# First expert's weights and x for h in 512 KB pieces behind weight tiles; last output pass split contiguously; gate products after both affinity transposes

## The chip, the cores and the metric

The kernel runs on one core of a Trainium2 chip. The metric is device microseconds of one execution; three executions of the kernel before took 1984.89 us in the median (1982.02 to 1988.62).

## The reference, cut to what matters

One trunk layer, all in float32: 256 latent and 256 context tokens of width 2048.

```python
mod = silu(c) @ w_mod + b_mod                       # shift, scale, gate for both halves of the layer
u = modulate(rmsnorm(tokens)) @ w_in                # 512 tokens, w_in 2048 x 11328
y = concat(ssd_branch(u[..., :D_SSM_IN]), short_conv_branch(u[..., D_SSM_IN:]))
h = x + g1 * (y @ w_out)[latent tokens]             # w_out 4096 x 2048
f = modulate(rmsnorm(h), sh2, sc2)
aff = softmax(f @ w_router)                         # 256 x 16
gates, idx = top_k(aff.T, 32)                       # each of 16 experts takes 32 tokens
xe = f[idx]
ye = (silu(xe @ w_gate) * (xe @ w_up)) @ w_down * gates   # per expert: 2048x1024, 2048x1024, 1024x2048
out = rmsnorm(h + g2 * scatter_add(ye, idx))
```

The expert weights are 402 MB of the 641 MB that the kernel moves.

## The kernel before, in words

**Dense part.** The products with w_in and w_out take their weights in tiles of 512 KB. `split_tile` (L84 to L113) makes one: it loads the tile into one of three `raw` buffers on SP's queue (L94), ScalarE casts it to a rounded half `whi` (L104), VectorE subtracts that to get `wlo` (L105), and TensorE makes three products of the halves (L339 and L336 for w_in, L826 and L883 for w_out), for a half tile of w_in 24 matmuls of 256 columns. After each tile's subtraction `split_tile` also issues what is due: postponed steps (`at_tick`), and rows of w_mod on the POOL queue at a set pace (`pace_`, 130 rows per 100 tiles, 105 from w_out on), each a 256 KB load `mraw` and one VectorE step (L406).

**Output projection.** The residual h (256 x 2048) starts as x, two loads of 1 MB (L752). Two passes over w_out give the columns 0 to 1024 and 1024 to 1536, with tokens as output rows (L826). The last pass gives columns 1536 to 2048 transposed (L878 to L886): there the weight tile is the operand that TensorE loads (LDWEIGHTS on PEld) and the token data move. Its four groups of 128 columns are every fourth column, so `split_tile` is called with `fours`: ScalarE and VectorE read the tile with a stride of four elements and write the halves grouped, and each matmul loads 128 neighbouring columns. Here too a tile has three products, 24 matmuls of 256 columns, and there are 16 tiles.

**Routing.** Logits `pl` (L891, L894), softmax per half of the tokens (`aff`), two transposes into `pa` (L919), and from it the search for each expert's 32 tokens on VectorE. Beside it TensorE makes `pt`, 16 small products that spread the gate g2 over rows (L923), which ScalarE copies to `g2r` (L925); four matmuls `warm` (L929) read `g2r`; the search's first result `bd` goes to TensorE in `pi` (L952).

**Experts.** 16 experts one after the other; each reads gate and up tiles of 2 MB (L1036, matmuls `gu` L1042) and down tiles (L1067, L1070). A tile's place comes from `wtile` and a list of slots: `ebig`, `abig`, `ebig`, four times `abig`, two `mbig` for the first nine, then a ring of the same. The first expert's tiles have slots that come free during the dense part (a slot `abig` holds halves of an activation until its last matmul), so they can be loaded before the experts begin: gate and up 0 to 3 alternating (below g0, u0, g1, u1, g2, u2, g3, u3), and 1 MB of the down weights (L1067, tile `e`).

**Order.** The engines run in the order that a scheduler writes down for each at build time, by readiness and by priority (`high_priority`); `issue_after` holds an instruction's place until another is placed. SP's queue starts its loads in that order: a load whose buffer isn't free holds all behind it.

Of the kernel before, what the change touches and what calls it, by code (L numbers as in the profile page):

```python
# [14 lines left out]
P = 128  # L15
# [11 lines left out]
RATE, RATE_OUT = 130, 105  # L27


@with_exitstack  # L30
def layer(ctx: ExitStack, tc: tile.TileContext, x, c, cx, c_ctx, w_mod, b_mod, norm_mix_w, w_in,
# [27 lines left out]
    def sbank(name="s"):  # L59
        return bank("s", 4, name)  # L60
# [22 lines left out]
    pace = [None]  # L83
# [4 lines left out]
    def split_tile(src, k0, c0, n, kn, fours=False):  # L88


        with tc.high_priority(offset=ahead[0]):
            w = raw_tile()
            wv = w.rearrange("p a b -> p (a b)")[:, 0:kn * n].rearrange("p (a b) -> p a b", a=kn)
            nc.sync.dma_start(wv, src.rearrange("(k p) c -> p k c", p=P)[:, k0:k0 + kn, c0:c0 + n])  # L94
            hi = wp.tile([P, 1024], F32R, name="whi", tag="whi", bufs=3)
            lo = wp.tile([P, 1024], F32R, name="wlo", tag="wlo", bufs=3)
            hv = hi[:, 0:kn * n].rearrange("p (a b) -> p a b", a=kn)
            lv = lo[:, 0:kn * n].rearrange("p (a b) -> p a b", a=kn)
            if fours:
                wf = wv.rearrange("p a (c i) -> p a i c", i=4)  # L100
                hf, lf = (v.rearrange("p a (i c) -> p a i c", i=4) for v in (hv, lv))
            else:
                wf, hf, lf = wv, hv, lv
            nc.scalar.copy(hf, wf)  # L104
            sub = nc.vector.tensor_tensor(lf, wf, hf.bitcast(F32), op=OP.subtract)  # L105
        tick[0] += 1
        with tc.issue_after(sub.ins):
            for x in sorted(y for y in due if y[0] <= tick[0]):
                due.remove(x)
                x[2]()  # L110
            if pace[0]:
                pace[0]()
        return hv, lv  # L113
# [313 lines left out]
    steps = mod_rows()  # L427
    n_rows, owed = [0], [0]

    def mod_rows_to(n):  # L430
        while n_rows[0] < n and next(steps, 0) is None:
            n_rows[0] += 1

    def pace_(rate, top):
        def fn():
            owed[0] += rate
            mod_rows_to(min(top, n_rows[0] + owed[0] // 100))
            owed[0] %= 100
        return fn
# [294 lines left out]
    yt = ebig().rearrange("p (k l) -> p k l", l=L)  # L734
    for j in range(1, 4):
        sc_block(j, gp, yt[:, 4 * j - 4:4 * j])
        for jj in ((0, 1) if j == 1 else (j,)):
            sq = squares(ysc[jj])
            if jj == 0:
                nc.gpsimd.tensor_copy(sums, sq)  # L740
            else:
                nc.gpsimd.tensor_tensor(sums, sums, sq, op=OP.add)
    mod_rows_to(12 * KT)
    pace[0] = pace_(RATE_OUT, 16 * KT)
    scx.close()
    h = hp_.tile([P, 2, D], F32, name="h")
# [4 lines left out]
    for t in range(2):  # L751
        nc.sync.dma_start(h[:, t], x[P * t:P * t + P, :])  # L752
# [122 lines left out]
    ov = [ob[i // 2][:, L * (i % 2):L * (i % 2) + L] for i in range(4)]  # L875
    for k0 in range(0, 2 * KT, 2):
        hi, lo = split_tile(w_out, k0, C3, 512, 2, True)
        end = k0 == 2 * KT - 2  # L878
        todo = [(i, x) for x in products(k0, 2, hi, lo) for i in range(4)]
        if end:  # L880
            todo.sort(key=lambda x: x[0])
        for i, (j, pi, yy, w) in todo:
            nc.tensor.matmul(ov[i], w[:, j, P * i:P * i + P], yy, start=(k0 + j == 0 and pi == 0 and i % 2 == 0),  # L883
                             stop=(end and j == 1 and pi == 2), skip_group_check=True)
# [28 lines left out]
    for t in range(2):  # L913
# [5 lines left out]
        nc.tensor.transpose(pa[0:NE, P * t:P * t + P], aff[:, t], ident)  # L919
    pt = sbank("pt")  # L920
    for q in range(4):
        for j in range(4):
            nc.tensor.matmul(pt[32 * q:32 * q + 32, P * j:P * j + P], g2c[:, 4 * q + j:4 * q + j + 1].to_broadcast([P, 32]),  # L923
                             ident, start=True, stop=True)
    nc.scalar.copy(g2r, pt)  # L925
# [73 lines left out]
    for e_ in range(NE):  # L999
# [32 lines left out]
        for k0 in range(0, KT, 4):  # L1032
            wt = []
            for w in (w_gate, w_up):
                t = wtile()
                nc.sync.dma_start(t.rearrange("p (a b) -> p a b", a=4),  # L1036
                                  w[e_].rearrange("(b p i) f -> p b i f", p=P, i=4)[:, k0 // 4])
                wt.append(t)
# [126 lines left out]
```

## Time and profile before

| | us |
|---|---|
| median of three executions | 1984.89 |
| the profiled execution | 1986.1 |
| its span | 1984.2 |
| dense part, to the end of the last pass | 0 to 1031 |
| routing, to the first expert's matmuls | 1031 to 1058 |
| experts | 1058 to 1984 |

PE was busy for 83% of the span, DVE for 46%, ACT for 27%, POOL for 9%; the DMA engines moved 641.11 MB, 323 GB/s over the span. The granted TensorE clock was 0.913 of full speed in the mean. The stages in the last three rows are read from the timeline of TensorE: the last matmul of L883, the first of L1042. Windows of the trace are read with four things in mind: how long an engine was busy, how many instructions it ran (so the spacing of like ones), what clock TensorE was granted, and what share of the 16 DMA engines was busy.

### The profile page before, as it was taken

How to read it: one execution, taken by the hardware profiler on the slowest of the kernel's cores; microseconds unless marked ns; L12 is line 12 of the kernel's file. 1: busy time of each engine (PE TensorE's matmuls, PEld its weight loads, DVE VectorE, ACT ScalarE, POOL GpSimd, SP SyncE). 2: the span in 40 equal slices, each digit the busy share in tenths (PEclk: the TensorE clock that was granted, in tenths of full speed). 3: DMA queues.
4: the chain of work that ended last, by engine and by line, in shares of the span. 5: the costliest groups of instructions: out<-in, count | busy, mean ns of one | idle time of the engine just before them, and what ended most of it. 6: DMA issues, size and time to landing. Idle time of an engine off the chain costs nothing.

```text
span 1984.2 us, 25476 instructions
## 1 busy us (share of the span) xinstructions
PE 1650.6 (83%) x10340; PEld 1014.4 (51%) x10340; DVE 914.7 (46%) x1387; ACT 532.2 (27%) x847; POOL 184.7 (9%) x314
## 2 busy tenths in 40 slices
PE   7999999999999799989988767667666767676686
PEld 5677997778699799867872111111111111111122
DVE  2457985778688688878743111111101111101113
ACT  4323554664666343434530000000000000000002
POOL 1000110212022233312100000000000000000000
PEclk9999999999999899999979887887878888988888
DMA  9964783546376989888768999999999999999996
GB/s 356 404 225 138 227 266 108 160 134 192 99 223 213 328 286 320 281 300 305 259 256 339 421 427 428 427 427 428 427 427 427 428 427 427 427 427 427 428 426 249
DMA packets 145813, 641.11 MB, mean 323 GB/s; under 512 B 16265, under 2 KB 34950, under 8 KB 120480
## 3 DMA queue, kind: packets, MB, share of 16 engines
q1 hardware_dynamic: 124528, 570.19, 73.9%
q0 software_dynamic: 20880, 68.25, 10.0%
q8 instruction: 81, 1.33, 0.3%
q10 hardware_dynamic: 288, 1.05, 0.1%
q14 instruction: 36, 0.29, 0.0%
HBM read 637.34 MB, written 2.10 MB: 322 GB/s over the span
## 4 chain that ended last, share of the span: by engine, by line
DMA 43%; PE 41%; issue 7%; DVE 5%; ACT 2%; POOL 1%; SPq 1%; POOLq 0%; ACTq 0%; DVEq 0%
DMA abig<-in_w_up_dram 21%; PE g L339 12%; PE g L336 11%; DMA ebig<-in_w_up_dram 6%; PE gu L1042 5%; DMA ebig<-in_w_down_dram 4%; DMA abig<-in_w_down_dram 3%; DMA mraw<-in_w_mod_dram 3%; DMA raw<-in_w_in_dram 2%; PE g L826 2%; DMA mwt<-in_w_down_dram 2%; PE yd L1075 2%; DMA mwt<-in_w_up_dram 2%; PE pm L248 1%; PE py L679 1%
## 5 line engine op out<-in xcount | busy, mean ns | idle before, releaser
L339 PE MATMUL g<-abig,whi 128*128 128x256 f32 x2048 | 373.2, 286 | 12.8 <-ACT whi L104 10.9
L105 DVE TENSOR_TENSOR wlo<-raw,whi 128x1024 fp32r<-128x1024 f32 x241 | 309.5, 1287 | 139.8 <-ACT whi L104 138.2
L104 ACT CAST whi<-raw 128x1024 fp32r<-128x1024 f32 x241 | 270.4, 1124 | 372.8 <-DMA raw<-in_w_out_dram 84.7
L1042 PE MATMUL gu<-abig,xe 128*32 128x512 f32 x1200 | 246.3, 778 | 117.8 <-DMA abig<-in_w_up_dram 106.1
L339 PEld LDWEIGHTS g<-abig,whi 128*128 128x128 f32 x2048 | 319.3, 193 | 19.0 <-ACT whi L104 11.2
L339 PE MATMUL g<-abig,wlo 128*128 128x256 f32 x1024 | 285.0, 286 | 2.1 <-DVE wlo L105 2.1
L1047 DVE SCALAR_TENSOR_TENSOR hid<-hid,gu 64x512 f32<-64x512 f32 x16 | 10.9, 679 | 482.2 <-ACT hid L1046 482.2
L336 PE MATMUL g<-abig,whi 128*128 128x512 f32 (+1 forms) x672 | 216.2, 400 | 3.7 <-ACT abig L320 2.0
L1046 ACT ACTIVATE hid<-gu 64x512 f32<-64x512 f32 x16 | 9.5, 591 | 722.9 <-PE gu L1042 722.9
L406 DVE SCALAR_TENSOR_TENSOR macc<-mraw,csl,macc 128x512 f32<-128x512 f32 x240 | 185.4, 773 | 28.1 <-DMA mraw<-in_w_mod_dram 26.0
L339 PEld LDWEIGHTS g<-abig,wlo 128*128 128x128 f32 x1024 | 194.5, 193 | 4.2 <-DVE wlo L105 3.2
L1042 PEld LDWEIGHTS gu<-abig,xe 128*32 128x32 f32 x1200 | 53.6, 133 | 277.1 <-DMA abig<-in_w_up_dram 135.7
L401 POOL DMA_DIRECT2D mraw<-in_w_mod_dram x256 | 138.1, 540 | 586.3 <-DVE macc L406 307.4
L1042 PE MATMUL gu<-ebig,xe 128*32 128x512 f32 x432 | 117.2, 801 | 45.5 <-DMA ebig<-in_w_up_dram 44.3
L1042 PE MATMUL gu<-mwt,xe 128*32 128x512 f32 x416 | 121.4, 862 | 33.8 <-DMA mwt<-in_w_up_dram 32.6
L336 PEld LDWEIGHTS g<-abig,whi 128*128 128x128 f32 (+1 forms) x672 | 122.8, 186 | 40.6 <-issue 9.2
L336 PE MATMUL g<-abig,wlo 128*128 128x512 f32 (+1 forms) x336 | 131.2, 394 | 0.0
L826 PE MATMUL g<-whi,abig 128*128 128x512 f32 x384 | 112.8, 397 | 6.1 <-ACT whi L104 5.4
L1089 DVE TENSOR_TENSOR m<-m,g 128x512 f32<-128x512 f32 x112 | 70.2, 683 | 77.5 <-PE g L1085 77.4
L1042 PEld LDWEIGHTS gu<-ebig,xe 128*32 128x32 f32 x432 | 24.5, 138 | 118.8 <-DMA ebig<-in_w_up_dram 58.6
L826 PEld LDWEIGHTS g<-whi,abig 128*128 128x128 f32 x384 | 72.8, 191 | 23.5 <-ACT whi L104 7.3
L1023 POOL DMA_DIRECT2D h<-in_final_norm_w_dram x1 | 0.6, 578 | 848.4 <-PE pt L1005 848.4
(339 smaller groups left out, 1801.5 us busy)
## 6 DMA issues: line engine op xcount, KB each, us to landing
raw<-in_w_in_dram SPq DMA_DIRECT2D x177, 512.0 KB, 4.7
abig<-in_w_up_dram SPq DMA_DIRECT2D x38, 2048.0 KB, 36.1
abig<-in_w_gate_dram SPq DMA_DIRECT2D x37, 2048.0 KB, 38.7
mraw<-in_w_mod_dram POOLq DMA_DIRECT2D x256, 256.0 KB, 4.8
abig<-in_w_down_dram SPq DMA_DIRECT2D x30, 2048.0 KB, 36.3
big<-in_w_mod_dram SPq DMA_DIRECT2D x32, 1024.0 KB, 10.5
raw<-in_w_out_dram SPq DMA_DIRECT2D x64, 512.0 KB, 5.2
mwt<-in_w_down_dram SPq DMA_DIRECT2D x16, 2048.0 KB, 34.7
```

The source lines that it names most:

```text
L104: nc.scalar.copy(hf, wf)
L105: sub = nc.vector.tensor_tensor(lf, wf, hf.bitcast(F32), op=OP.subtract)
L248: nc.tensor.matmul(pm[32 * q:32 * q + 32, o:o + n], cst[:, k], w[:, k - k0], start=(k < 4), stop=(k >= KT - 4), skip_group_check=True)
L336: nc.tensor.matmul(banks[ct][0:ncol], st, a[q][:, kk], start=beg, stop=end)
L339: nc.tensor.matmul(banks[ct // 2][0:ncol, o:o + L], st, a[q][:, kk, L:2 * L], start=beg and ct % 2 == 0, stop=end, skip_group_check=True)
L401: nc.gpsimd.dma_start(w, w_mod[P * k:P * k + P, c0:c0 + 512])
L406: nc.vector.scalar_tensor_tensor(acc, w, cs, acc, op0=OP.mult, op1=OP.add)
L679: nc.tensor.matmul(oo, l, r, start=(i == 0), stop=(i == 3), skip_group_check=True)
L826: nc.tensor.matmul(ob[nn * t + m], yy[:, P * t:P * t + P], w[:, j, 512 * m:512 * m + 512], start=(k0 + j == order[0] and pi == 0), stop=(k ...
L1042: nc.tensor.matmul(gu[32 * q:32 * q + 32], xe[:, k], wt[q // 2][:, 1024 * kk + 512 * (q % 2):1024 * kk + 512 * (q % 2) + 512], start=(k == ...
L1075: nc.tensor.matmul(yd[32 * q:32 * q + 32], hidT[:, j, 32 * (c // 2):32 * (c // 2) + 32], parts[i][:, 512 * q:512 * q + 512], start=(c == 0 ...
L1089: nc.vector.tensor_tensor(av, h[:, t, 512 * q:512 * q + 512] if e_ == 0 else av, pc[q], op=OP.add)
```

## The change

A generator `first_weights` issues the first expert's seven tiles g0, u0, g1, u1, g2, u2, g3 in quarters of 512 KB, after g0 the 1 MB of down weights in two halves and x for h in four pieces of 512 KB: 34 pieces in all. They are issued by `feed`, which `split_tile` calls with `issue_after(load.ins)`, so each stands behind the load of the weight tile before it: from the twelfth tile of the short convolution's last three blocks on, half a piece per tile up to 10, then from the eighth tile of w_out's first pass on up to 18, and from the eighth of the last pass on one piece per tile up to 34; `first_to(34)` issues what is left. The slots are the same, and so are the bytes. `counted` makes the pace of w_mod's rows usable for both.

```diff
...
-    def split_tile(src, k0, c0, n, kn, fours=False):
+    def split_tile(src, k0, c0, n, kn):
...
-            nc.sync.dma_start(wv, src.rearrange("(k p) c -> p k c", p=P)[:, k0:k0 + kn, c0:c0 + n])
+            load = nc.sync.dma_start(wv, src.rearrange("(k p) c -> p k c", p=P)[:, k0:k0 + kn, c0:c0 + n])
...
-            if fours:
-                wf = wv.rearrange("p a (c i) -> p a i c", i=4)
-                hf, lf = (v.rearrange("p a (i c) -> p a i c", i=4) for v in (hv, lv))
-            else:
-                wf, hf, lf = wv, hv, lv
-            nc.scalar.copy(hf, wf)
-            sub = nc.vector.tensor_tensor(lf, wf, hf.bitcast(F32), op=OP.subtract)
+            nc.scalar.copy(hv, wv)
+            sub = nc.vector.tensor_tensor(lv, wv, hv.bitcast(F32), op=OP.subtract)
...
+        with tc.issue_after(load.ins):
+            if feed[0]:
+                feed[0]()
...
+    def first_weights():
+        for n, slot in enumerate([ebig, abig, ebig] + [abig] * 4):
+            first.append(abig(F32) if slot is abig else slot())
+            src = (w_gate, w_up)[n % 2][0].rearrange("(b p i) f -> p b i f", p=P, i=4)[:, n // 2]
+            for i in range(4):
+                nc.sync.dma_start(first[n][:, 1024 * i:1024 * i + 1024], src[:, i])
+                yield
+            if n == 0:
+                first8.append(e8())
+                src = w_down[0, 4 * P:6 * P].rearrange("(p i) n -> p i n", i=2)[:, 0]
+                for i in range(2):
+                    nc.sync.dma_start(first8[0][:, 1024 * i:1024 * i + 1024], src[:, 1024 * i:1024 * i + 1024])
+                    yield
+                for t in range(2):
+                    for c in range(0, D, 1024):
+                        nc.sync.dma_start(h[:, t, c:c + 1024], x[P * t:P * t + P, c:c + 1024])
+                        yield
...
+    at_tick(12, lambda: feed.__setitem__(0, feed_(FEED, 10)))
...
+    at_tick(8, lambda: feed.__setitem__(0, feed_(FEED, 18)))
...
-    for t in range(2):
-        nc.sync.dma_start(h[:, t], x[P * t:P * t + P, :])
+    first_to(10)
...
+    at_tick(8, lambda: feed.__setitem__(0, feed_(FEED_LAST, 34)))
...
-        hi, lo = split_tile(w_out, k0, C3, 512, 2, True)
+        hi, lo = split_tile(w_out, k0, C3, 512, 2)
...
-            nc.tensor.matmul(ov[i], w[:, j, P * i:P * i + P], yy, start=(k0 + j == 0 and pi == 0 and i % 2 == 0),
+            nc.tensor.matmul(ov[i], in_fours(w[:, j])[:, i], yy, start=(k0 + j == 0 and pi == 0 and i % 2 == 0),
...
-        nc.tensor.transpose(pa[0:NE, P * t:P * t + P], aff[:, t], ident)
-    pt = sbank("pt")
...
+        turned = nc.tensor.transpose(pa[0:NE, P * t:P * t + P], aff[:, t], ident)
+    with tc.issue_after(turned.ins):
+        pt = sbank("pt")
...
```

SP's queue in the tail of w_in, before: `raw` are weight tiles of 512 KB, 128x4096 is 2 MB, 128x2048 is 1 MB.

```order
L94 DMA raw<-in_w_in_dram 128x2x512 x101
L752 DMA h<-in_x_dram 128x2048
L94 DMA raw<-in_w_in_dram 128x2x512
L752 DMA h<-in_x_dram 128x2048
L1036 DMA ebig<-in_w_gate_dram 128x4096
L1067 DMA e_10260<-in_w_down_dram 128x2048
L94 DMA raw<-in_w_in_dram 128x2x512 x50
```

The same place after; 128x1024 is 512 KB.

```order
L95 DMA raw<-in_w_in_dram 128x2x512 x101
L744 DMA ebig<-in_w_gate_dram 128x1024
L95 DMA raw<-in_w_in_dram 128x2x512
L744 DMA ebig<-in_w_gate_dram 128x1024 x3
L95 DMA raw<-in_w_in_dram 128x2x512
L750 DMA e_6341<-in_w_down_dram 128x1024 x2
L95 DMA raw<-in_w_in_dram 128x2x512 x2
L754 DMA h<-in_x_dram 128x1024
L95 DMA raw<-in_w_in_dram 128x2x512 x2
```

Of the 5 MB that stood around one weight tile, 1.5 MB of g0 now stand between two tiles, the 1 MB of down weights behind the next, and the four pieces of h (the first is shown) each behind two more.

SP's queue in the second half of the last pass, before: u1, g2, u2 and g3 in 2 MB.

```order
L94 DMA raw<-in_w_out_dram 128x2x512 x25
L1036 DMA abig<-in_w_up_dram 128x4096
L94 DMA raw<-in_w_out_dram 128x2x512 x3
L1036 DMA abig<-in_w_gate_dram 128x4096
L94 DMA raw<-in_w_out_dram 128x2x512 x3
L1036 DMA abig<-in_w_up_dram 128x4096
L94 DMA raw<-in_w_out_dram 128x2x512
L1036 DMA abig<-in_w_gate_dram 128x4096
```

After:

```order
L744 DMA abig<-in_w_up_dram 128x1024
L95 DMA raw<-in_w_out_dram 128x2x512 x2
L744 DMA abig<-in_w_gate_dram 128x1024 x2
L95 DMA raw<-in_w_out_dram 128x2x512
L744 DMA abig<-in_w_gate_dram 128x1024
L95 DMA raw<-in_w_out_dram 128x2x512
L744 DMA abig<-in_w_gate_dram 128x1024
L95 DMA raw<-in_w_out_dram 128x2x512
L744 DMA abig<-in_w_up_dram 128x1024 x4
L744 DMA abig<-in_w_gate_dram 128x1024 x4
```

The last weight tile stood behind u2; now u2 and g3 stand behind it, and pieces of g2 between the last four tiles. (In the first w_out pass, u0 and g1 likewise turn from two loads of 2 MB into pieces: u0's four still in a row, g1's behind the next tiles as 2, 1 and 1.)

TensorE's order in the routing, before:

```order
L919 MATMUL pa<-ident,aff 16x128
L923 MATMUL pt<-ident,mods 32x128 x15
L919 MATMUL pa<-ident,aff 16x128
L923 MATMUL pt<-ident,mods 32x128
L929 MATMUL warm<-g2r,ident 128x512 x4
L952 MATMUL pi__10081<-bd,ones 128x128
```

After:

```order
L950 MATMUL pa<-ident,aff 16x128 x2
L955 MATMUL pt<-ident,mods 32x128 x16
L961 MATMUL warm<-g2r,ident 128x512 x4
L984 MATMUL pi__10113<-bd,ones 128x128
```

All 16 gate products now stand behind the second transpose; `warm` and `pi` stay behind them.

## Rows read from the trace of the kernel before

**Rows 1.** The profile page: the chain that ended last, shares of the span by engine.

```profile
DMA 43%; PE 41%; issue 7%; DVE 5%; ACT 2%; POOL 1%; SPq 1%; POOLq 0%; ACTq 0%; DVEq 0%
```

**Rows 2.** Stretches: PE, PEld, DVE, ACT, POOL busy (instructions); PE clock; DMA share; GB/s.

```profile
1100.00:1950.00 850.00, 592.82 (x3340) 147.34 (x3340) 123.49 (x224) 24.04 (x46) 0.58 (x1) 0.84 1.01 426
1052.00:1062.00 10.00, 8.61 (x58) 2.46 (x54) 2.50 (x8) 0.59 (x1) 0.00 (x0) 0.83 0.12 48
```

**Rows 3.** Waits of SP's queue from 980 to 1064: waited-for, total us, times, longest.

```profile
SPq L1067 <- PE gu L1042: 27.8, 1, 27.8
```

**Rows 4.** Timeline of SP's queue from 632: start, us, line, load.

```profile
635.58 0.42 SPq L1036 DMA_DIRECT2D ebig<-in_w_gate_dram  x1
636.61 0.39 SPq L94 DMA_DIRECT2D raw<-in_w_in_dram  x1
```

**Rows 5.** Timelines of ACT, DVE and PE at 657; in brackets idle time before, releaser.

```profile
657.19 1.04 ACT L104 CAST whi<-raw 128x1024 fp32r<-128x1024 f32 x1 [14.64 <-DMA raw<-in_w_in_dram]
658.26 1.23 DVE L105 TENSOR_TENSOR wlo<-raw,whi 128x1024 fp32r<-128x1024 f32 x1 [11.45 <-ACT whi L104]
658.28 1.22 PE L339 MATMUL g<-abig,whi 128*128 128x256 f32 x4 [10.95 <-ACT whi L104]
```

**Rows 6.** Stretches around the burst at 635, columns as in rows 2.

```profile
648.00:658.00 10.00, 0.00 (x0) 0.00 (x0) 0.00 (x0) 0.81 (x1) 0.00 (x0) 0.59 0.99 385
658.00:663.00 5.00, 4.68 (x20) 4.39 (x21) 4.70 (x6) 2.32 (x3) 1.08 (x2) 0.50 0.52 150
632.00:664.00 32.00, 21.01 (x154) 20.32 (x153) 19.99 (x32) 7.85 (x11) 8.29 (x12) 0.79 0.88 332
664.00:760.00 96.00, 95.12 (x794) 94.92 (x793) 81.79 (x102) 38.31 (x42) 32.57 (x54) 1.00 0.90 303
```

**Rows 7.** Timelines of SP's queue and PE around g1's load at 860.

```profile
859.98 0.33 SPq L1036 DMA_DIRECT2D ebig<-in_w_gate_dram  x1
874.45 1.60 PE L826 MATMUL g<-whi,abig 128*128 128x512 f32 x4 [4.58 <-ACT whi L104]
```

**Rows 8.** Stretches of the last pass, columns as in rows 2.

```profile
967.00:1031.00 64.00, 56.48 (x418) 54.30 (x417) 42.49 (x38) 33.40 (x25) 4.84 (x9) 0.90 0.68 244
1000.00:1008.00 8.00, 6.58 (x31) 6.37 (x32) 7.89 (x6) 4.46 (x4) 0.00 (x0) 0.58 0.88 343
1024.00:1031.00 7.00, 5.15 (x23) 4.94 (x24) 2.86 (x3) 1.10 (x3) 0.00 (x0) 0.59 0.00 0
```

**Rows 9.** Groups of PE, 967 to 1031: busy us, mean ns | idle before, releaser.

```profile
L883 PE MATMUL g<-abig,whi 128*128 128x256 f32 x255 | 42.0, 301 | 4.4 <-ACT whi L104 4.4
L883 PE MATMUL g<-abig,wlo 128*128 128x256 f32 x128 | 24.1, 305 | 2.8 <-DVE wlo L105 2.8
```

**Rows 10.** Timelines of SP's queue, ACT and DVE at the last two tiles.

```profile
1013.23 0.34 SPq L1036 DMA_DIRECT2D abig<-in_w_up_dram  x1
1013.66 0.67 SPq L94 DMA_DIRECT2D raw<-in_w_out_dram  x1
1022.30 1.99 ACT L104 CAST whi<-raw 128x1024 fp32r<-128x1024 f32 x1 [6.97 <-DMA raw<-in_w_out_dram]
1024.32 1.98 DVE L105 TENSOR_TENSOR wlo<-raw,whi 128x1024 fp32r<-128x1024 f32 x1 [6.11 <-ACT whi L104]
```

**Rows 11.** Timeline and groups of weight loads: strided (L861) and contiguous (L883, L626).

```profile
975.51 0.56 PEld L861 LDWEIGHTS pt<-ident,h 128*128 128x128 f32 x4
975.98 0.20 PEld L883 LDWEIGHTS g<-abig,whi 128*128 128x128 f32 x1
...
L883 PEld LDWEIGHTS g<-abig,whi 128*128 128x128 f32 x256 | 37.4, 208 | 5.7 <-ACT whi L104 4.8 <-issue 0.8
L626 PEld LDWEIGHTS pt<-ident,xs 128*128 128x128 f32 x64 | 8.0, 141 | 5.1 <-issue 3.2 <-PE g L336 0.5 <-PE g L339 0.2
```

**Rows 12.** Timeline of PE in the routing.

```profile
1044.15 3.70 PE L929 MATMUL warm<-g2r,ident 128*128 128x512 f32 x8 [0.67 <-ACT g2r L925]
1048.86 0.34 PE L952 MATMUL pi__10081<-bd,ones 16*128 16x128 f32 x1 [1.01 <-DVE bd L949]
```

More of the change, by code (lines that the diff above doesn't have):

```diff
@@ L27 @@
 RATE, RATE_OUT = 130, 105
+FEED, FEED_LAST = 50, 100
 @with_exitstack
@@ L81, in at_tick @@
         due.append((tick[0] + n, seq[0], fn))
-    pace = [None]
+    pace, feed = [None], [None]
     def raw_tile():
         return wp.tile([P, 2, 512], F32, name="raw", tag="raw", bufs=3)
-    def split_tile(src, k0, c0, n, kn, fours=False):
+    def split_tile(src, k0, c0, n, kn):
         with tc.high_priority(offset=ahead[0]):
@@ L425, in mod_rows, with counted, to, pace_ @@
                 yield
[L427 to L439, printed above, removed]
+    def counted(steps):
+        done, owed = [0], [0]
+        def to(n):
+            while done[0] < n and next(steps, 0) is None:
+                done[0] += 1
+        def pace_(rate, top):
+            def fn():
+                owed[0] += rate
+                to(min(top, done[0] + owed[0] // 100))
+                owed[0] %= 100
+            return fn
+        return to, pace_
+    mod_rows_to, pace_ = counted(mod_rows())
     pace[0] = pace_(RATE, 12 * KT)
@@ L727, in ebig, with e8 @@
         return ep.tile([P, 4096], F32, name="ebig", tag="ebig")
+    def e8():
+        return ep.tile([P, 2048], F32, name="e8", tag="e8", bufs=1)
+    first, first8 = [], []
+    h = hp_.tile([P, 2, D], F32, name="h")
+    def first_weights():
[15 more added lines that the diff above has]
+                        yield
+    first_to, feed_ = counted(first_weights())
     scx = ExitStack()
@@ L744, in layer @@
     pace[0] = pace_(RATE_OUT, 16 * KT)
+    at_tick(8, lambda: feed.__setitem__(0, feed_(FEED, 18)))
     scx.close()
-    h = hp_.tile([P, 2, D], F32, name="h")
     oh = hp_.tile([P, 2, NE * CAP], F32, name="oh")
@@ L918, in layer @@
         nc.vector.tensor_scalar(aff[:, t], aff[:, t], st[:, t, 1:2], None, op0=OP.mult)
-        nc.tensor.transpose(pa[0:NE, P * t:P * t + P], aff[:, t], ident)
-    pt = sbank("pt")
[L921 to L925, printed above, removed]
+        turned = nc.tensor.transpose(pa[0:NE, P * t:P * t + P], aff[:, t], ident)
+    with tc.issue_after(turned.ins):
+        pt = sbank("pt")
+        for q in range(4):
+            for j in range(4):
+                nc.tensor.matmul(pt[32 * q:32 * q + 32, P * j:P * j + P],
+                                 g2c[:, 4 * q + j:4 * q + j + 1].to_broadcast([P, 32]), ident, start=True, stop=True)
+        nc.scalar.copy(g2r, pt)
     warm = sbank("warm")
@@ L980, in m8 @@
         return mw.tile([P, 2048], F32, name="m8", tag="m8")
-    def e8():
-        return ep.tile([P, 2048], F32, name="e8", tag="e8", bufs=1)
-    slots = [ebig, abig, ebig] + [abig] * 4 + [mbig] * 2
+    first_to(34)
+    slots = [mbig] * 2
     ring = [ebig] * 2 + [abig] * 5 + [mbig] * 2
@@ L991, in wtile @@
         nw[0] += 1
+        if i < len(first):
+            return first[i]
+        i -= len(first)
         f = slots[i] if i < len(slots) else ring[(i - len(slots)) % len(ring)]
@@ L1034, in layer @@
             for w in (w_gate, w_up):
[L1035 to L1038, printed above, removed]
+                loaded = nw[0] < len(first)
+                wt.append(wtile())
+                if not loaded:
+                    nc.sync.dma_start(wt[-1].rearrange("p (a b) -> p a b", a=4),
+                                      w[e_].rearrange("(b p i) f -> p b i f", p=P, i=4)[:, k0 // 4])
             for kk in range(4):
@@ L1064, in layer @@
                 if e_ == 0 and c in (1, 2):
-                    parts = [m8(), m8()] if c == 1 else [e8(), wtile()[:, 0:2048]]
-                    for i in range(2):
+                    parts = [m8(), m8()] if c == 1 else [first8[0], wtile()[:, 0:2048]]
+                    for i in range(c - 1, 2):
                         nc.sync.dma_start(parts[i], src[:, i])
```

## The prediction

> **What bounds the kernel now.** I first read the chain that ended last: DMA 43%, PE 41% [rows 1], so two resources bound it in turn, and the question is where each does. The stretches by time tell it. From 1100 to 1950 the DMA engines are busy all the time (share 1.01) at 426 GB/s while PE works 593 of 850 us; from 1052 to 1062 their share is 0.12 [rows 2]. In between lies a start: SP's queue waits 27.8 us in one piece for the first expert's matmuls [rows 3], since every tile buffer is full. Thus the expert phase moves a fixed number of bytes at a rate that PE doesn't set, and it can begin only when the dense part and the routing are through. **What the change takes from these two moves the end one for one; in the expert phase itself it moves no byte and no instruction.** The dense part is PE's: at full clock 794 matmuls stand in 95.12 us of 96, 0.12 us apart [rows 6]. Its losses are the places where PE waits for a weight tile that stands in SP's queue behind something large, and the slow clock afterwards.
>
> **The burst at 635.** g0 (2 MB) is issued at 635.58 just ahead of a weight tile at 636.61 [rows 4]; with the two loads of x and the down weights it is 5 MB around one tile, as the order before shows. The DMA engines run full (0.99, 385 GB/s) from 648 to 658, and no matmul runs in these 10 us; then come 20 matmuls in 5 us at a granted clock of 0.50, that is 1.2 GHz [rows 6]. At 0.12 us each these would take 2.4 us, so the clock costs 2.3 of the 4.68, and the idle time at the tile itself is 10.95 [rows 5]; together 13.2 us. After the change that tile has two pieces fewer than g0 and neither h nor down weights ahead of it, 3.1 MB less (before: 2.1 of x, 2.1 of g0, 1.05 of down weights and its own 0.5; after: what is left of g0 and one more tile). At 385 GB/s that is 8.2 us sooner. The rest follows over the next ten tiles, and there the room is small: the share was 0.90 from 664 to 760 at 303 GB/s [rows 6]. Ten tiles of 24 matmuls at 0.12 are 29 us; 3.1 MB in these are 107 GB/s more, 410 in all, over the 385 that the full engines moved. Some 0.7 MB, 2 us, are late and lie in the queue ahead of weight tiles, which three raw buffers can cover in part. I count the clock's 2.3 as mostly regained and the 2 us as lost: **8 us**. Bounds: 3 (the pieces crowd the tiles behind them) and 13.2 (all of it).
>
> **g1 at 860.** A load of 2 MB at 859.98, and PE idles 4.58 us at the tile behind it [rows 7]. In its new place 1 MB less stands before the next weight tile: 1.05 MB at 385 GB/s are **2.7 us**. Bounds 0 and 4.6. (u0's quarters stay in a row; I saw no idle time of PE there to win.)
>
> **The last pass.** 64 us, of which PE works 56.5 [rows 8]. Idle at whi 4.4, at wlo 2.8 [rows 9]; these are two places, the ninth tile near 1000 and the last near 1024, with about half of each sum. Slow clock behind each: from 1000 to 1008 at 0.58, 31 matmuls in 6.58 us, 2.9 more than at 0.12 each; from 1024 to 1031 at 0.59, 23 in 5.15, 2.4 more [rows 8]. Sum 12.5. Three things of the change act here. The ninth tile's successors stand behind 1 MB of u1 and not 2: 2.7 us sooner, against about 2.2 of idle time. The last tile, issued at 1013.66 behind u2 at 1013.23 [rows 10], no longer waits for u2's 2 MB (5.4 us) but for two or three pieces of g2 (2 to 3 us). And the split no longer reads with a stride: 1.99 and 1.98 us [rows 10] become 1.04 and 1.23, what the same operations take on the contiguous tile at 657 [rows 5], so whi comes 0.95 and wlo 1.7 us sooner after the load. That covers both idle times if the tiles keep pace with a PE that is ahead of its old times; I leave one slow stretch of 2.9 standing: **9.6 us**. Bounds 4 (only the split helps) and 12.5. ScalarE and VectorE lose 16 x 0.95 and 16 x 0.75 us of work beside it, which nobody waits for.
>
> **The stride moves to the weight load.** 384 loads (256 and 128, [rows 9]) now read every fourth column. The trace has such loads: the transposes of L861 load h with the same stride, four in a row, and the next load starts 0.47 us after the first [rows 11], 0.118 apart, the spacing that the 256-column matmuls have anyway. So I cost it at nothing, hidden by the matmul it overlaps. Contiguous transposes record 141 ns for a load, L883's own loads 208 [rows 11], so by records the room is there too. Against it: if strided loads do not overlap, the spacing is matmul 0.1075 (256 columns at 2.4 GHz) plus load 0.118, 0.225 us, and the pass takes 384 x 0.225 + 4.4 (its other matmuls) = 90.8 us.
>
> The Trainium skill speaks against this edit ("Advanced Engine Details and Errata", Memory Cachelines): SBUF has lines of 16 bytes, and an access pattern that takes a new line for each element pays. A stride of four float32 is just that. The trace agrees for ScalarE, 1.99 us strided against 1.04 [rows 5, 10], a factor 1.9. By that factor the loads of the pass would stand 0.22 us apart, about rival B's spacing and time, below; L861's row speaks against it.
>
> **Gate products.** They now follow the second transpose. The second transpose no longer waits behind 15 of them, which frees the affinities earlier, but `pi` stands behind `warm` on TensorE, and `warm` behind the copy to g2r [rows 12], which now comes later. `pi` started 1.01 us after `warm` ended because the search was late; this idle time is all that can be won: **0.8**, bounds 0 and 1.0. A loss is possible if the products take longer as one block; their time is the same, so I see none.
>
> **SP's queue.** 24 more issues of some 0.4 us [rows 4] in a queue that spends most of its time waiting: 0. They stand behind a weight tile's load, so a piece whose slot isn't free (u1, g2, u2, g3 need a freed `abig`) still blocks the tiles behind it, as before.
>
> **Sum.** 8 + 2.7 + 9.6 + 0.8 = 21.1 us. Against the profiled execution, 1986.1 - 21.1 = 1965.0; the median of three is 1.2 lower, so 1963.8, say 1964.
>
> **Rivals.** *A: the stalls only move.* The engines' share from 632 to 760 averages 0.895 (0.88 x 32 and 0.90 x 96 [rows 6]); taking 10 us out of this leaves it at 0.97, and late tiles at other places can eat the gain. If a third is left of the first term and half of the last pass: 3 + 1 + 5 + 0.5 = 9.5, some 1975. For it: the small room; against: the weight tiles now come first, and w_mod's rows can yield. *B: strided weight loads slow the last pass* and the kernel ends slower. At 0.225 us the pass is 26.9 us longer instead of 9.6 shorter; with the other 11.5 gained the time is 1984.9 + 15.4 = 2000. It decides from a spacing of 0.185 on (384 x 0.185 + 4.4 = 64 + 11.5). For it: ScalarE's factor; against: the row of L861. *C: the pieces do not spread*, since the scheduler and not `feed` places them: the order after still has three of g0 in a row, so this is in part so, and is counted in the terms. What remains of it would give A's time.
>
> **How the numbers follow.** 74% for the forecast, 17% for A with C, 9% for B. This kernel's runs tell a difference of 0.3%, 6 us, from none. The forecast is faster throughout; of A 12 points are faster and 5 within 0.3%; of B 7 points are slower, 2 within 0.3%: 0.86, 0.07, 0.07. Upper bounds summed are 31.3 (1984.9 - 31.3 = 1953.6), lower ones 7 (1977.9). The range takes both and so nearly all of A: 1953 to 1979; B is left out.
>
> **What would show it.** PE's idle time near 647 to 658 shrinks to under 5 us, with no stretch of 0.50 behind it; the last pass takes 52 to 56 us with matmuls 0.12 apart and splits of 1.04 and 1.23; `pi` follows `warm` at once; the DMA engines are full from some 20 us earlier, and the time from the first `gu` to the end stays 926 us. I am wrong if the spacing in the last pass exceeds 0.13, if idle times of 5 us appear at tiles between 660 and 760, or if the expert phase begins earlier and ends no sooner.

## The result and the profile after

The changed kernel takes 2006.19 us in the median of four executions (2005.08 to 2012.11), the kernel before 1983.91 beside it (1982.02 to 1988.62): a ratio of 1.0115, with a 95% interval of 1.0088 to 1.0142. It is slower by 22 us, outside the range of 1953 to 1979. The profiled execution has a span of 2003.2 us (2005.08 in all), 19.0 more than before.

Four marks on TensorE's timeline say where the 19.0 us are. The summary of one line gives the first and the last start of its matmuls; here it is for the last pass (L883 before, L914 after) and for the first matmul of the experts (L1042, L1076). First the kernel before:

```profile
L883 PE MATMUL g<-abig,whi x256: 278/283/416, 967.3 to 1031.0; 128*128 128x256 f32 x128
L1042 PE MATMUL gu<-ebig,xe x432: 592/628/1062, 1058.1 to 1928.3; 128*32 128x512 f32 x144
```

Then the changed kernel (after the count: shortest, median and longest in ns):

```profile
L914 PE MATMUL g<-abig,whi x256: 282/395/508, 958.0 to 1051.8; 128*128 128x256 f32 x128
L1076 PE MATMUL gu<-ebig,xe x432: 592/636/1063, 1078.1 to 1948.2; 128*32 128x512 f32 x144
```

| stretch | before, us | after, us | difference |
|---|---|---|---|
| start to the last pass | 967.3 | 958.0 | -9.3 |
| last pass, first to last matmul start | 63.7 | 93.8 | +30.1 |
| to the first expert's matmul | 27.1 | 26.3 | -0.8 |
| to the end of the span | 926.1 | 925.1 | -1.0 |

So three of four stretches moved about as forecast, and one did the opposite. (In the third the size agrees by chance: from the first transpose of the affinities to the first expert's matmul both kernels take 19.1 us, and the 0.8 stands ahead of it.) The stretches of the changed kernel by time, with the columns of rows 2, show that it is not a wait: in the last pass PE has no idle time at all and its full clock, and does in 96 us what it did in 64 [rows 8].

```profile
647.00:652.00 5.00, 4.51 (x24) 4.22 (x24) 3.39 (x4) 0.76 (x2) 1.61 (x3) 0.66 1.03 390
957.00:1053.00 96.00, 96.00 (x433) 94.76 (x431) 31.07 (x40) 19.56 (x25) 4.31 (x8) 1.00 0.48 161
1120.00:1970.00 850.00, 580.10 (x3350) 145.76 (x3344) 123.14 (x224) 24.04 (x46) 0.58 (x1) 0.84 1.01 426
```

The third row answers to the first of rows 2: the expert phase is as full of transfers as before, 426 GB/s, and begins later. What grew is the weight load. Its groups between 975 and 1053 (busy us, mean ns), to be held against the L883 row of rows 11:

```profile
L914 PEld LDWEIGHTS g<-abig,whi 128*128 128x128 f32 x212 | 53.1, 329 | 0.8 <-issue 0.8
L914 PEld LDWEIGHTS g<-abig,wlo 128*128 128x128 f32 x104 | 27.4, 330 | 0.0
L872 PEld LDWEIGHTS pt<-ident,h 128*128 128x128 f32 x6 | 0.8, 212 | 0.0
```

A record of 208 ns has become one of 329. And PE's timeline has groups like this one, eight matmuls in 2.03 us, and the next one beginning 1.87 us after the first of them began:

```profile
1002.08 1.09 PE L914 MATMUL g<-abig,wlo 128*128 128x256 f32 x4
1003.01 2.03 PE L914 MATMUL g<-abig,whi 128*128 128x256 f32 x8
1004.88 1.09 PE L914 MATMUL g<-abig,wlo 128*128 128x256 f32 x4
```

1.87 / 8 = 0.234 us from one matmul to the next, where 0.12 were forecast. 384 times 0.234 are 90 us; with the pass's other small matmuls, the 93.8.

### The profile page after: what moved, and what is told of

The parts are those of the page before. It is cut to its first block, busy times and chain, and to the rows that moved or that the text cites. A ratio compares the mean times of both kernels' runs of the same rounds, so it can differ in the third digit from the quotient of the medians.

```text
span 2003.2 us, 25499 instructions
## 1 busy us (share of the span) xinstructions
PE 1671.1 (83%) x10340; PEld 1047.1 (52%) x10340; DVE 900.9 (45%) x1387; ACT 515.9 (26%) x847; POOL 183.9 (9%) x314
## 4 chain that ended last, share of the span: by engine, by line
DMA 44%; PE 39%; issue 7%; DVE 5%; ACT 2%; SPq 1%; POOL 1%; DVEq 0%; ACTq 0%; POOLq 0%
DMA abig<-in_w_up_dram 15%; PE g L335 11%; PE g L338 10%; DMA ebig<-in_w_up_dram 7%; DMA mwt<-in_w_up_dram 5%; DMA mwt<-in_w_down_dram 5%; PE gu L1076 4%; DMA mraw<-in_w_mod_dram 3%; DMA raw<-in_w_in_dram 3%; DMA ebig<-in_w_down_dram 3%; PE g L856 2%; DMA abig<-in_w_down_dram 2%; PE g L914 2%; PE yd L1109 2%; DVE wlo L101 2%
## 5 line engine op out<-in xcount | busy, mean ns | idle before, releaser
L101 DVE TENSOR_TENSOR wlo<-raw,whi 128x1024 fp32r<-128x1024 f32 x241 | 295.7, 1230 | 168.2 <-ACT whi L100 167.0
L100 ACT CAST whi<-raw 128x1024 fp32r<-128x1024 f32 x241 | 254.0, 1055 | 381.9 <-DMA raw<-in_w_in_dram 87.2
L1076 PE MATMUL gu<-abig,xe 128*32 128x512 f32 x1200 | 247.0, 799 | 109.2 <-DMA abig<-in_w_up_dram 101.4
L1076 PEld LDWEIGHTS gu<-abig,xe 128*32 128x32 f32 x1200 | 54.6, 139 | 274.6 <-DMA abig<-in_w_up_dram 133.7
L1076 PE MATMUL gu<-ebig,xe 128*32 128x512 f32 x432 | 116.1, 812 | 53.7 <-DMA ebig<-in_w_up_dram 50.0
L1076 PE MATMUL gu<-mwt,xe 128*32 128x512 f32 x416 | 109.9, 791 | 41.4 <-DMA mwt<-in_w_up_dram 32.6
L1076 PEld LDWEIGHTS gu<-ebig,xe 128*32 128x32 f32 x432 | 24.2, 138 | 122.0 <-DMA ebig<-in_w_up_dram 64.3
```

The lines of the kernel that those rows point to most:

```text
L100: nc.scalar.copy(hv, wv)
L101: sub = nc.vector.tensor_tensor(lv, wv, hv.bitcast(F32), op=OP.subtract)
L1076: nc.tensor.matmul(gu[32 * q:32 * q + 32], xe[:, k], wt[q // 2][:, 1024 * kk + 512 * (q % 2):1024 * kk + 512 * (q % 2) + 512], start=(k == ...
```

## The experiments

My theory after the result was L: the strided weight load costs the whole loss. The rival P: the pieces or their order cost it, and the slow matmuls only fill time that would be lost anyway.

**e1_split: the stride back on the split.** In the changed kernel, ScalarE and VectorE read with the stride again, and TensorE loads neighbouring columns:

```diff
-            nc.scalar.copy(hv, wv)
-            sub = nc.vector.tensor_tensor(lv, wv, hv.bitcast(F32), op=OP.subtract)
+            if fours:
+                wf = wv.rearrange("p a (c i) -> p a i c", i=4)
+                hf, lf = (v.rearrange("p a (i c) -> p a i c", i=4) for v in (hv, lv))
...
-            nc.tensor.matmul(ov[i], in_fours(w[:, j])[:, i], yy, ...
+            nc.tensor.matmul(ov[i], w[:, j, P * i:P * i + P], yy, ...
```

> The changed kernel with one part undone: in the last pass ScalarE and VectorE again read the tile with a stride and TensorE loads 128 neighbouring columns. Theory L (the strided weight load costs the whole loss, since it isn't hidden behind the matmul): matmuls of the last pass 0.12 us apart instead of 0.234, the pass 52 to 62 us instead of 94, and the time 1963 to 1975 us. Rival P (the 512 KB pieces or their order cost it): the pass may get shorter, but idle time of PE or a later start of the DMA engines takes its place, and the time stays over 1985.

1971.97 us (1969.72 to 1974.56), ratio 0.9927 (0.9899 to 0.9956). The last pass runs from 962.5 to 1016.7, 54.2 us. L holds.

**e2_load: the stride on the weight load alone, in the kernel before.** The same edit of split and matmul as in the change, and nothing else of it.

> The kernel before with one part of the change alone: contiguous split in the last pass, strided weight load. Theory L: the pass takes 94 us as in the changed kernel instead of 64, and nothing else moves: 2012 to 2016 us. Rival P: the strided load costs only beside the pieces' traffic, and the time stays within 6 us of 1984.

2014.87 us (2010.39 to 2017.22), ratio 1.0137 (1.0106 to 1.0168). The pass takes 93.8 us as in the changed kernel, with the loads in 2 MB as they were:

```profile
L883 PE MATMUL g<-abig,whi x256: 283/395/508, 965.2 to 1059.0; 128*128 128x256 f32 x128
```

P falls: with none of the pieces, this edit alone brings the pass of the kernel before from 63.7 us to the same 93.8.

**e3_plain: no stride on either side.** In the changed kernel, `w[:, j, P * i:P * i + P]` for the matmul, and nothing else.

> The changed kernel with both split and weight load contiguous: the columns of the last pass's four groups are then the wrong ones (neighbouring instead of every fourth), the work is otherwise the same. Theory L: matmuls 0.12 us apart, the pass 50 to 56 us, 1960 to 1967 us; what it is below the kernel with the strided split is what that split costs there, at most 5 us. Rival P: over 1985 us.

1965.65 us (1964.64 to 1966.55), ratio 0.9895 (0.9868 to 0.9921), the pass 50.2 us. This is the time that I had forecast for the change (1964), with the one assumption made true that was false: a weight load that costs nothing. Between it and e1 lie 6 us (4.0 of them in the pass), more than the at most 5 expected: VectorE takes 2.06 us for a strided wlo in e1, ScalarE 2.09 for a strided whi, and PE waits for wlo for 1.8 us in the pass. Where the rest of the 4.0 went isn't shown.

```profile
L106 DVE TENSOR_TENSOR wlo<-raw,whi 128x1024 fp32r<-128x1024 f32 x15 | 30.8, 2057 | 9.3 <-ACT whi L105 9.1
L105 ACT CAST whi<-raw 128x1024 fp32r<-128x1024 f32 x14 | 29.3, 2092 | 13.7 <-DMA raw<-in_w_out_dram 10.1 <-PE g L919 2.0 <-DVE htmp L868 1.0
L919 PE MATMUL g<-abig,wlo 128*128 128x256 f32 x128 | 21.8, 285 | 1.8 <-DVE wlo L106 1.8
```

**e4_loads: what a strided load costs by itself.** 240 matmuls ahead of the last pass, in groups of 24, the stride of the weight operand and the number of moving columns varied:

```diff
+    for i in range(24):
+        nc.tensor.matmul(mb[:, 0:256], yf[:, 0:512].rearrange("p (c i) -> p i c", i=4)[:, 0],
+                         yt4[:, 0:256], start=True, stop=True)
...
```

> The kernel before with 240 matmuls put ahead of the last pass, whose results nothing reads: ten groups of 24, the weight operand in float32r contiguous with 128, 256 and 512 moving columns, with stride 2 and 256, with stride 4 and 128, 256 and 512, with stride 8 and 256, then float32 transposes with contiguous and with stride 4 weights. Theory L1 (a strided load takes about 0.13 us and can't overlap with the matmul): stride 4 apart by 0.18, 0.234 and 0.34 us for 128, 256 and 512 columns. Theory L2 (a strided load overlaps but takes 0.234 us by itself): 0.234, 0.234 and 0.23 to 0.25. Stride 1 in either: 0.06 to 0.09, 0.117, 0.22. If the transposes at stride 4 stay at 0.118 apart, the type of the operand makes the difference to the row that the prediction took.

One run, 2029.56 us, of which the added matmuls are some 42. The timeline of PE's weight loads, one row for each group of 24, so that the step from row to row divided by 24 is the spacing. In order: stride 1 with 128, 256 and 512 moving columns; stride 2 with 256; stride 4 with 128, 256 and 512; stride 8 with 256; then float32 transposes at stride 1 and 4. (The last group has no row behind it; its last load starts at 967.7.)

```profile
925.65 2.77 PEld L863 LDWEIGHTS g<-abig 128*128 128x128 f32 x24
928.35 2.94 PEld L865 LDWEIGHTS g<-abig 128*128 128x128 f32 x24
931.22 5.36 PEld L867 LDWEIGHTS g<-abig 128*128 128x128 f32 x24
936.61 3.06 PEld L869 LDWEIGHTS g<-abig 128*128 128x128 f32 x24
939.60 5.68 PEld L871 LDWEIGHTS g<-abig 128*128 128x128 f32 x24
945.18 5.74 PEld L873 LDWEIGHTS g<-abig 128*128 128x128 f32 x24
950.82 5.74 PEld L875 LDWEIGHTS g<-abig 128*128 128x128 f32 x24
956.48 5.88 PEld L877 LDWEIGHTS g<-abig 128*128 128x128 f32 x24
962.30 2.64 PEld L879 LDWEIGHTS g<-ident,h 128*128 128x128 f32 x24
964.91 3.01 PEld L881 LDWEIGHTS g<-ident,h 128*128 128x128 f32 x24
```

| weight operand | moving columns | us apart |
|---|---|---|
| float32r, stride 1 | 128 / 256 / 512 | 0.112 / 0.120 / 0.225 |
| float32r, stride 2 | 256 | 0.125 |
| float32r, stride 4 | 128 / 256 / 512 | 0.233 / 0.235 / 0.236 |
| float32r, stride 8 | 256 | 0.243 |
| float32 transpose, stride 1 / 4 | 128 | 0.109 / 0.122 |

At stride 4 the spacing doesn't depend on what the matmul does beside it: that is L2, a load that overlaps but takes 0.234 us itself (L1 would give 0.18 for 128 and 0.34 for 512 columns). Behind 512 columns it would have been almost hidden, behind 256 it is not. And the last two rows are the trap: the transposes, the one kind of strided load that the trace of before shows [rows 11], don't pay for their stride.

**e8_loads: what sets that price.** The same with 128 moving columns: float32r at stride 2, 3, 4, at stride 4 with 64 weight columns; float32 in a plain matmul at stride 1 and 4 (48 loads each, two for a matmul); float32 transposes at stride 2 and 4.

> The kernel before with 192 matmuls put ahead of the last pass, whose results nothing reads, 128 moving columns each, in eight groups of 24: float32r weights with stride 2, 3 and 4, stride 4 with 64 weight columns, float32 weights in a plain matmul with stride 1 and 4, and float32 transposes with stride 2 and 4. If the line of 16 bytes sets the cost, stride 3 (12 bytes) lies between 0.11 and 0.23 us, and 64 columns at stride 4 take about half of 0.23. If it is the number of columns alone or a fixed price, 64 columns take as long as 128. If the transposes' own mode makes stride 4 cheap, the plain float32 matmul at stride 4 is more than 0.1 us longer than at stride 1 for each of its weight loads.

```profile
921.68 2.92 PEld L863 LDWEIGHTS g<-abig 128*128 128x128 f32 x24
924.52 4.67 PEld L865 LDWEIGHTS g<-abig 128*128 128x128 f32 x24
929.07 5.72 PEld L867 LDWEIGHTS g<-abig 128*128 128x128 f32 x24
934.70 2.98 PEld L869 LDWEIGHTS g<-abig 128*64 128x64 f32 x24
937.57 6.83 PEld L871 LDWEIGHTS g<-ident,h 128*128 128x128 f32 x48
944.32 11.28 PEld L873 LDWEIGHTS g<-ident,h 128*128 128x128 f32 x48
955.39 3.07 PEld L875 LDWEIGHTS g<-ident,h 128*128 128x128 f32 x24
958.37 3.02 PEld L877 LDWEIGHTS g<-ident,h 128*128 128x128 f32 x24
```

Steps divided by 24, or 48: 0.118 at stride 2, 0.190 at stride 3, 0.235 at stride 4, 0.120 with half the columns at stride 4; plain float32 0.141 at stride 1 and 0.231 at stride 4; transposes 0.124 at stride 2. But the groups did not all have the same clock. Stretches of this trace, with the columns of rows 2: the groups at stride 4 with 128 and with 64 columns, plain float32 at stride 1, the end of that group alone, and plain float32 at stride 4.

```profile
929.07:934.70 5.63, 5.63 (x26) 5.63 (x26) 0.00 (x0) 0.00 (x0) 0.00 (x0) 0.50 0.27 102
934.70:937.57 2.87, 2.87 (x26) 2.87 (x25) 0.00 (x0) 0.00 (x0) 0.00 (x0) 0.50 0.00 0
937.57:944.32 6.75, 6.75 (x51) 6.75 (x49) 0.00 (x0) 0.00 (x0) 0.00 (x0) 0.78 0.01 2
941.50:944.30 2.80, 2.80 (x27) 2.80 (x26) 0.00 (x0) 0.00 (x0) 0.00 (x0) 1.00 0.00 0
944.32:955.39 11.07, 11.07 (x50) 11.07 (x49) 0.00 (x0) 0.00 (x0) 0.00 (x0) 1.00 0.00 0
```

The strided load took 0.235 us at a granted clock of 0.50, as it did at full clock in e4 (0.236 with 512 moving columns), so its price didn't follow the clock. With half the columns the group ran at 0.50 throughout, and 0.120 is at most what it takes at full clock: the price is not a fixed one. It has its full size at stride 4 and 8, is in between at stride 3 (0.190, at a clock of 0.76 in the mean) and can hardly be seen at stride 2. Plain float32 at stride 1 took 0.141 as a mix of two clocks; its last 26 loads, at full clock, stood about 0.11 apart, so stride 4 costs it about 0.12 for each load, over the 0.1 that was set as the mark. The transposes, all at full clock in both runs, pay 0.013 to 0.015: it is their mode and not the type of the operand that makes them cheap. The run is one, 2020.94 us.

This is the rule of the Trainium skill that the prediction weighed and put aside ("Advanced Engine Details and Errata", Memory Cachelines: 16-byte lines, at least two hits on one for full speed). Two float32 of a 16-byte line are used at stride 2, one at stride 4. The runs agree with it for the weight loads of matmuls: 0.118 against 0.235 us. They don't for those of transposes: 0.124 at stride 2 and 0.122 at stride 4.

**e5_pairs: the stride shared between both sides.** If stride 2 is free for the load, and pairs of neighbours are free for ScalarE and VectorE, then the regrouping can be split: the halves are written as two groups of pairs, and the load picks every second column.

```diff
+            if pairs:
+                wv = w.rearrange("p a (c q i) -> p q (a c) i", q=2, i=2)
+                hv, lv = (v.rearrange("p (q c i) -> p q c i", q=2, i=2) for v in (hi, lo))
             nc.scalar.copy(hv, wv)
             sub = nc.vector.tensor_tensor(lv, wv, hv.bitcast(F32), op=OP.subtract)
+            if pairs:
+                hv, lv = (v.rearrange("p (q a c i) -> p a q i c", q=2, a=2, i=2) for v in (hi, lo))
...
-            nc.tensor.matmul(ov[i], in_fours(w[:, j])[:, i], yy, ...
+            nc.tensor.matmul(ov[i], w[:, j, i // 2, i % 2], yy, ...
```

> The changed kernel with the regrouping shared between both sides: ScalarE and VectorE read runs of two neighbouring elements every four, and TensorE's weight load reads every second column. Theory L2 with the cost setting in between stride 2 and stride 4: matmuls of the last pass 0.117 us apart, as with contiguous loads; the splits lie between 1.04 and 1.99 us. If the reads in pairs run at full rate (1.04 and 1.23 us), the time is that of the kernel with both sides contiguous, 1964 to 1968 us; if they cost what the stride of four costs, 1970 to 1974. Rival (a stride 2 load does cost in the pass, with loads of two kinds of tile in turn): spacing over 0.13 us and over 1975 us.

1966.74 us (1963.31 to 1971.7), ratio 0.9903 (0.9886 to 0.992). The pass runs from 962.5 to 1012.8, 50.3 us, and the splits take 1.14 and 1.22 us in the mean:

```profile
L104 DVE TENSOR_TENSOR wlo<-raw,whi 128x1024 fp32r<-128x1024 f32 x15 | 18.4, 1224 | 17.3 <-ACT whi L103 17.2
L103 ACT CAST whi<-raw 128x1024 fp32r<-128x1024 f32 x14 | 16.0, 1143 | 19.3 <-DMA raw<-in_w_out_dram 15.0 <-PE g L919 4.3
```

That is e3's time within the spread, with the right columns: VectorE pays nothing for reading pairs (1.23 contiguous [rows 5]), ScalarE 0.1 us.

**e6_pairs_gate: the gate products back.** e5 with the 16 products where they stood before, free to stand between the two transposes.

> The paired kernel with the gate products where they stood before: between the two transposes of the affinities. By the prediction's term the routing becomes 0.8 us longer (0 to 1.0), which the time can't show and the trace can: pi's idle time behind warm is back at about 1 us. Rival: it becomes shorter, since warm and pi start earlier with the copy.

1966.1 us (1965.88 to 1968.71), not to be told from e5's. In the trace, from the first transpose of the affinities (`pa`) to the first expert's matmul: 20.13 us in e6 (1019.31 to 1039.44), 18.68 in e5 (1020.77 to 1039.45), 1.4 us less with the later place. In the changed kernel nothing is won: 19.09 (1059.01 to 1078.10) against 19.10 before (1039.03 to 1058.13). One pair of traces doesn't size so small a term, since the stretch goes with the time of the products: 3.5 to 4.5 us for the 32 records in the eight traces with the later place. Without them it is 14.2 us in seven of these eight (14.6 in the changed kernel) and 15.1 in four of the six with the old place (15.4 in e6, 15.8 in e4). So the later place wins 0.9 us, near the 0.8 forecast. In the changed kernel this went to the clock: its products took 4.49 us at a granted clock of 0.51, against 4.01 at 0.64 before, and its last `pi` 0.76 against 0.45. `pi` follows `warm` at once, as forecast, where it came 1.01 us later before [rows 12] and 0.78 later in e6:

```profile
1059.56 4.49 PE L955 MATMUL pt<-ident,mods 128*32 128x128 f32 x32
...
1064.72 3.70 PE L961 MATMUL warm<-g2r,ident 128*128 128x512 f32 x8 [0.68 <-ACT g2r L957]
1068.35 0.48 PE L984 MATMUL pi__10113<-bd,ones 16*128 16x128 f32 x2
```

**e7_before_pairs: the paired split alone.** The kernel before with e5's edit of split and matmul.

> The kernel before with the paired split alone, its loads in 2 MB and 1 MB as they were. By the prediction's terms only what the split itself holds up goes: the last pass 64 to about 58 to 61 us (wlo's idle time 2.8 and some of the slow clock), 1979 to 1983 us. Rival (the split's length was the main loss of the last pass, and the 2 MB loads cost nothing there): the pass at 52 to 54 us, 1973 to 1976 us.

1975.27 us (1973.47 to 1980.08), ratio 0.995 (0.9932 to 0.9967). The rival was right: the pass takes 54.4 us (967.1 to 1021.5) with the 2 MB loads as they stood. With the pieces alone (e1) it takes 54.2, with both 50.3. The 13 us that can be won in this pass have two causes, and either cure takes some 9 of them.

**e9_first10, e10_slow, e11_later: which pieces pay.** All from e5, which ran again beside them as e12_pairs_again. e9 feeds only the ten pieces at 635 and leaves the other six tiles in 2 MB; e10 halves the pace in w_out's first passes (25 per 100 tiles); e11 begins there twelve tiles later:

```diff
-    at_tick(8, lambda: feed.__setitem__(0, feed_(FEED, 18)))
+    at_tick(8, lambda: feed.__setitem__(0, feed_(25, 18)))        # e10
...
+    at_tick(20, lambda: feed.__setitem__(0, feed_(FEED, 18)))     # e11
```

> The paired kernel with only the burst at 635 in pieces (g0, the first half MB loads of the down weights, x); u0, g1, u1, g2, u2, g3 in 2 MB where they stood in the kernel before. Theory S (each place pays for itself): 8 us are gained up to the first product with w_out, 9.5 in the last pass from the paired split (54.5 us long), 1 in the routing: 1966 to 1968 us, the same as the paired kernel, since the pieces cost 2 to 3 us in w_out's first two passes (161 to 162 us against 159) and gain 4 in the last. Rival (the later pieces carry part of the gain): 1971 to 1976 us.

> The paired kernel with u0 and g1 fed at one piece per four tiles of w_out instead of two tiles; in the order the eight pieces now stand between 23 tiles, 2, 1, 1, 1, 1, 1, 1 at a time. Theory (the 4 MB close together around 845 to 870 hold up the tiles behind them whether in pieces or not): PE's idle time between 850 and 885 falls from 7 us to 3 to 5, w_out's first two passes from 162 to 157 to 160 us, and the time is 2 to 4 us below the paired kernel's. Rival (that idle time is VectorE's, which normalises and splits the last activations then): no difference.

> The paired kernel with the same pace but u0 and g1 begun twelve tiles later than in the changed kernel, all eight pieces singly and two tiles apart, away from the place where VectorE normalises the last activations. Theory: 2 to 4 us below the paired kernel, as with the slow feed. Rival: the idle time moves to the later tiles and nothing is gained.

> The paired kernel again, as the measure for the three others on the same chip: 1964 to 1969 us.

| run | us | ratio to before (95%) | w_out's first two passes | last pass |
|---|---|---|---|---|
| before | 1986.19 | | 159.3 | 63.7 |
| e12_pairs_again | 1963.48 | 0.9896 (0.9881 to 0.9912) | 158.9 | 50.3 |
| e9_first10 | 1971.56 | 0.9929 (0.9916 to 0.9942) | 163.1 | 53.9 |
| e10_slow | 1961.98 | 0.9884 (0.987 to 0.9899) | 156.8 | 50.3 |
| e11_later | 1961.94 | 0.9879 (0.9865 to 0.9894) | 157.8 | 50.4 |

e9 falls on its rival's side: without the later pieces it is 8 us over e12. Of these, 3.6 stand in the last pass and are shown: with pieces there and a split that isn't slow the pass took 50.2 to 50.4 us in every trace. The 4.2 in the two passes ahead are not: e5 and e6, with e12's feed, took 162.2 and 162.3 us there against e9's 163.1. e10 and e11 are the fastest in the median, and faster than both kernels of the case, but only 1.5 us below e12, where 2 to 4 were expected, and their intervals overlap e12's. The traces have the effect: the two passes took 158.9 to 162.3 us in all six traces with the faster feed, and PE was busy for 33.2 and 32.4 us from 850 to 885, against 29.4 in e12 and 26.9 to 30.5 in the nine other traces (e4 and e8 left out):

```profile
850.00:885.00 35.00, 33.21 (x141) 27.11 (x142) 28.37 (x35) 13.56 (x16) 6.74 (x13) 0.95 0.89 313
850.00:885.00 35.00, 29.43 (x117) 22.31 (x118) 26.00 (x32) 11.03 (x13) 6.21 (x12) 0.95 0.89 319
```

The first row is e10, the second e12.

## Why the prediction was wrong, step by step

**The strided weight load: the step that failed.** It was costed at nothing, "hidden by the matmul it overlaps", from L861's row: four strided loads 0.118 us apart [rows 11]. The row was read rightly and stood for something else. L861 is a float32 transpose, and by e4 and e8 a transpose is the one case in which stride 4 costs next to nothing (0.109 to 0.122 us), while the same stride in a matmul's load takes 0.235. Forecast for the step: 0. Measured: 43.6 us, 93.8 for the pass against 50.2 in e3, which differs in this alone. The second argument, that L883's loads had records of 208 ns against 141 for the contiguous transposes "so by records the room is there too", rested on the same mistake: it compared a matmul with a transpose.

**Rival B** was therefore the case, at a chance of 9%. Its size was near (2000 against 2006, a pass of 90.8 against 93.8), but its mechanism was not: it added load and matmul, 0.225, where the load alone takes 0.235 and the matmul runs beside it. With 512 moving columns such a sum gives 0.33 (twice 0.1075, and 0.118), and e4 has 0.236.

**The burst at 635: right.** Forecast 8 us, bounds 3 to 13.2. The first product with w_out starts at 808.0, 806.7, 807.9, 808.0 and 803.2 in before, e2, e7, e4 and e8, and between 797.4 and 801.3 in the changed kernel, e1, e3, e5, e6, e9, e10, e11 and e12: 7.7 us between the means. Idle time of PE at the tile went from 10.95 [rows 5] to 2.41, and the clock fell for a short stretch only, 24 matmuls in 4.51 us (the first of the stretches above):

```profile
647.38 1.16 PE L338 MATMUL g<-abig,whi 128*128 128x256 f32 x4 [2.41 <-ACT whi L100]
```

**g1 at 860: not there.** Forecast 2.7 us, bounds 0 to 4.6. From the first product with w_out to the last pass took 159.3 us before (158.5 and 159.2 in e2 and e7), 160.6 in the changed kernel, and 158.9 to 162.3 in the five others with the same feed: nothing won, and up to 3 us lost. The 4.58 us of idle time [rows 7] came apart into three smaller ones (in the changed kernel):

```profile
868.51 1.20 PE L856 MATMUL g<-whi,abig 128*128 128x512 f32 x4 [1.64 <-ACT whi L100]
872.77 1.20 PE L856 MATMUL g<-whi,abig 128*128 128x512 f32 x4 [0.89 <-ACT whi L100]
881.61 0.74 PE L856 MATMUL g<-wlo,abig 128*128 128x512 f32 x2 [1.38 <-DVE wlo L101]
```

That was rival A's mechanism, at one place: 4 MB within 22 us delay the tiles behind them in pieces as well as whole. Spread out (e10, e11) the same pieces leave the two passes at 156.8 and 157.8 us. What whole loads would have cost here once TensorE comes 8 us earlier is open: e9 has 163.1, one trace, just above the range of those with pieces.

**The last pass: undersized, and shared.** Forecast 9.6 of at most 12.5. With loads that cost nothing it is 13.4 (e5: 50.3 against 63.7), over the bound, which was worked out from PE's idle and slow time alone. The three causes were not to be added: the split's length alone (e7) takes away 9.3 us and the pieces alone (e1) 9.5. I set the split by itself at 4, "bounds 4 (only the split helps)". Why each takes away so much, the traces show. Before, PE waits for the split for 7.2 us at two tiles (the tenth, which the prediction calls the ninth, and the last), and the clock falls to 0.58 and 0.59 behind them [rows 8], by the prediction's sum another 5.3 us. In e7 waits of 2.6 us are left, at the thirteenth tile and at the last, and the clock stays at 1.00 through the whole pass, as in e1. The slow clock goes with either cure, and only once. The first two of e7's waits, and the stretch behind them:

```profile
1006.72 0.76 PE L883 MATMUL g<-abig,whi 128*128 128x256 f32 x4 [0.66 <-ACT whi L102]
1007.98 0.76 PE L883 MATMUL g<-abig,wlo 128*128 128x256 f32 x4 [0.50 <-DVE wlo L103]
1007.00:1015.00 8.00, 7.50 (x62) 7.30 (x62) 4.72 (x6) 2.14 (x2) 0.00 (x0) 1.00 0.88 329
```

**Gate products: right, and not to be seen.** Forecast 0.8, bounds 0 and 1.0. Without the products' own time the stretch is 0.9 us shorter with the later place, by fourteen traces; in the changed kernel a slower clock in the routing took this back, and the stretch is as long as before.

**The end.** What the dense part and the routing win or lose moves the end one for one: right, within 3 us. The time from the first expert's matmul to the end of the span is 926.1 us before, 925.1 after, and 926.0 to 929.1 in the other twelve traces. With the load's price gone the sum stands: 1965 (e3) for 1964. That it stands so exactly is luck. Against the trace of before, e3's has 7.9 us less up to the first product with w_out, 1.5 more in the first two passes, 13.5 less in the last, 2.3 less in the routing and 1.1 more in the experts, together the 21.1 of the forecast; the last pass and the routing gave 5.4 more than their terms, and g1's place and the experts 5.3 less.

## What to carry to other kernels

A row bears on an edit only if it is the same instruction in the same mode; a transpose is no stand-in for a matmul's weight load. Before moving a stride from one engine to another, ask how long the receiving operation is and what covers it: a 128-column load at stride 4 has only a 256-column matmul to hide behind, and half the stride on each side cost next to nothing on either. Where two causes stall the same stretch, price the cure of each alone, since their gains don't add.

## What the runs showed of the hardware

A float32r weight load of 128 columns with stride 4 or 8 takes 0.235 to 0.243 us, whatever the matmul beside it moves, and at a granted clock of 0.50 (e8) as at 1.00 (e4); with stride 3 0.190; with stride 2 it hides behind 128 columns (0.118). In float32 transposes stride 4 costs 0.013 us, in plain float32 about 0.12 for each load. VectorE and ScalarE read pairs of neighbours out of every four at full speed or nearly (1.22 and 1.14 us for 128 x 1024), single elements at 2.06 and 2.09. Loads in pieces did not spare the tiles behind them by being in pieces: with u0 and g1 within 22 us PE was busy for 28.2 to 29.4 us of the 35 from 850 to 885, with the same pieces spread out or later for 33.2 and 32.4. In the time of the runs that is 1.5 us, within the spread.
